# A hybrid decoder layer on one core: the base-rotor table stored with its 16 positions innermost, a left sum of the first feed-forward moved to VectorE, and side work every 2.75 matmul triples

## The chip, the core and the metric

The kernel runs on one core of a Trainium2 chip. The core has five engines with queues of their own: TensorE (PE in the profile; its weight loads are PEld), VectorE (DVE), ScalarE (ACT), GpSimd (POOL) and SyncE (SP), which here issues the DMAs. Each engine executes its instructions strictly in the order in which the program issues them and waits on semaphores for the others. The metric is the device time of one execution in microseconds, as a median over runs; lower is better.

## The reference, cut to what matters

One layer with 1024 tokens and width 1024: a feed-forward half-step, a mixer (short convolution and a diagonal state-space model side by side), a second feed-forward half-step, a final norm.

```python
h = modulate(rms_norm(x, ffn1_norm[l]), sh1, sc1)
x = x + 0.5 * g1[:, None, :] * swiglu(h, ffn1_w_gate[l], ffn1_w_up[l], ffn1_w_down[l])

h = modulate(rms_norm(x, mix_norm[l]), sh2, sc2)
proj = h @ w_in[l]
...
y_ssm = s5_mixer(u, lambda_re[l], lambda_im[l], log_dt[l], ssm_b_re[l], ssm_b_im[l],
                 ssm_c_re[l], ssm_c_im[l], ssm_d[l], glu_w[l], glu_b[l])
...
x = x + g2[:, None, :] * (y_mix @ w_out[l])

h = modulate(rms_norm(x, ffn2_norm[l]), sh3, sc3)
x = x + 0.5 * g3[:, None, :] * swiglu(h, ffn2_w_gate[l], ffn2_w_up[l], ffn2_w_down[l])
return rms_norm(x, final_norm)
```

Two things that depend on no activation are needed later: the modulation vectors, `silu(cond) @ w_mod + b_mod`, and the tables of the state-space model, among them the rotors, powers of `exp(i * lambda_im * dt)` for each of 32 groups of channels, with 64 states.

## The kernel before

**Arithmetic.** Every matmul of two matrices is done as three in reduced format: each operand is split into a high part and a low part, and `mm3` (line 306) issues high times high, high times low, low times high. Such a triple is the unit of the kernel's own clock. The activation's split is a cast on ScalarE and a subtraction on VectorE (`split_act`); a weight's split (tile `w`, from the loaded tile `raw`) is the same pair over 1024 columns.

**The first feed-forward.** The 2816 hidden columns are handled in 11 groups of 256 (names `fa0` to `fa10`), the 1024 tokens in two halves of 512. Groups 0 to 5 are direct: `gate_up` (line 1015) computes for each of two tiles the gate product (`fa2g`, ...) and the up product (`fa2u`, ...) for both halves, 64 triples in all; `gu_evac` takes them out of PSUM (Silu on ScalarE into `sg`, the product `af` on VectorE, then the split `a`). `down_both` (line 1027) multiplies by the down weights, 32 triples (`fa2d`, ...): 16 output tiles of six matmuls each, each taken out by one VectorE instruction that adds it to the residual `x`. All these products share six PSUM banks (`mm_ps`, line 229), so a new tile waits until an older one has been taken out. Groups 6 to 10 use a scheme with seven block products in place of eight (`seven`). It needs sums of activation blocks, made by `combos` (line 483): S1, S2 and S3 with VectorE additions during group 5, then, once group 5's projections are issued, the fourth left sum S4 = A12 − S2. In the code before, the three additions of S4 for each of four tiles (two recombinations of a split pair, `f12` and `s2`, and their difference) run on GpSimd, and the split into the tile `h1S` is done by ScalarE and VectorE as elsewhere. On GpSimd also run the sums of weight blocks (tile `sums`, lines 158 to 160).

**Side work.** While groups 0 to 4 run, a generator `side1` (line 997) is stepped by the clock: `Clock.tick` (line 67) is called at each triple and takes one step of the generator every `period` triples. The period is 4 at first, 3 during `gate_up` of groups 1 to 4 and 8 during their `down_both`. The generator first runs `ssm_base` (line 772): small VectorE instructions that make `lam`, `pw`, `tab` and two rotor tables, `base` (tile `rb`, 16 positions by 32 groups) and `step` (tile `rs`, 8 positions by 32 groups), by repeated doubling. Then come eight batches of `ssm_batch` (line 916), four channel groups each: products `bb`, `cl`, `bl` on VectorE, two groups of small matmuls on TensorE (`kp` and `tp`, which read `cl` and `bl`), copies to DRAM, three `mod_block`s (two reductions of a loaded 1024-wide tile `wm` each, on VectorE), and four products of `step` with `base` (`rot` and `rott`) with a sum for each pair. Each step ends at a `yield`.

**Order.** The program is written in this order, but a scheduler in the framework decides where each instruction stands in its engine's queue; after that the order is fixed. So the clock's steps decide roughly, and the scheduler exactly, what stands ahead of an eviction on VectorE or of a matmul on TensorE.

**Pools.** `sb` lives through the side work, `sb1` only through `ssm_base`; the pool `bp` of the batches takes the room of `sb1` afterwards.

Of the kernel before, what the change touches and what calls it, by code (L numbers as in the profile page):

```python
# [13 lines left out]
F32 = mybir.dt.float32  # L14
# [40 lines left out]
class Clock:  # L55
# [1 line left out]


    def __init__(self, period):
        self.now, self.period, self.n = 0, period, 0  # L60
        self.due, self.side = [], deque()

    def after(self, ticks, fn):
# [3 lines left out]
    def tick(self):  # L67
        self.now += 1
        while self.due and self.due[0][0] <= self.now:
            self.due.pop(0)[2]()  # L70
        if self.now % self.period == 0:
            self.step()

    def step(self):
# [142 lines left out]
def hymba_layer(ctx: ExitStack, tc, x_d, wm1_d, wmod_d, gu1_d, gs1_d, wd1_d, win_d, wout_d, glu_d, gu2_d, gs2_d, wd2_d, cols_d, cond_d, lam_d, bc_d, out_d):  # L217
# [265 lines left out]
    def combos(act, name, homes, engine=None):  # L483

        blocks.clear()
        while act[1] is None or len(act[1]) < KT:
            yield
        (a11, a12), (a21, a22) = [(act[h][:4], act[h][4:]) for h in range(2)]
        blocks.update(A11=a11, A12=a12, A22=a22, S1=[], S2=[], S3=[], S4=[])
        G_ = engine or V  # L490
        for k in range(4):
            f22, f21, f11 = whole(a22[k], f"f22_{k}", V), whole(a21[k], f"f21_{k}", V), whole(a11[k], f"f11_{k}", V)
            V.tensor_tensor(out=f22[:], in0=f21[:], in1=f22[:], op=ALU.add)
            blocks["S1"].append(split_act(f22[:], f"{name}S1_{k}", homes[0]))
            yield
            V.tensor_tensor(out=f21[:], in0=f11[:], in1=f21[:], op=ALU.subtract)
            V.tensor_tensor(out=f11[:], in0=f22[:], in1=f11[:], op=ALU.subtract)
            blocks["S2"].append(split_act(f11[:], f"{name}S2_{k}", homes[1]))
            yield
            blocks["S3"].append(split_act(f21[:], f"{name}S3_{k}", homes[2]))  # L500
            yield
        while "free" not in blocks:
            yield
        for k in range(4):
            f12, s2 = whole(a12[k], f"f12_{k}", G_), whole(blocks["S2"][k], f"s2_{k}", G_)
            yield
            G_.tensor_tensor(out=f12[:], in0=f12[:], in1=s2[:], op=ALU.subtract)
            blocks["S4"].append(split_act(f12[:], f"{name}S4_{k}", homes[3]))
            yield
# [262 lines left out]
    def ssm_base(sb1):  # L772
# [100 lines left out]
        V.tensor_tensor(out=r8[:], in0=w[0], in1=w[0], op=ALU.mult)  # L873
        V.tensor_scalar(out=ro[1][hi], in0=ro[1][hi], scalar1=-1.0, scalar2=None, op0=ALU.mult)
        cur = (ro[0], ro[1])
        base = [sb.tile([P, 16, G], F32, tag=f"rb{i}", name=f"rb{i}") for i in range(2)]
        step = [sb.tile([P, 8, G], F32, tag=f"rs{i}", name=f"rs{i}") for i in range(2)]

        def doubled(nm):
# [12 lines left out]
        for tab, cnt in ((base, 16), (step, 8)):  # L892
            V.memset(tab[0][:, 0, :], 1.0)
            V.memset(tab[1][:, 0, :], 0.0)
            n = 1
            while n < cnt:
                by = tuple(a.unsqueeze(1).to_broadcast([P, n, G]) for a in cur)
                cmul(sb1, 
                    tuple(t[:, n : 2 * n, :] for t in tab), tuple(t[:, 0:n, :] for t in tab), by, [P, n, G], f"t{cnt}_{n}"
                )  # L900
                doubled(f"c{cnt}_{n}")
                yield
                n *= 2
        yield
        zero = sb1.tile([CH, 112], F32, name="zero")
        V.memset(zero[:], 0.0)
        mk4 = mk_d[:].rearrange("b p (g c) -> p b g c", g=GB)
        for t in range(1, TAU):
            for b in range(NB):
# [1 line left out]
                    mk4[t * CH : (t + 1) * CH, b, :, 0 : t * CH],  # L911
                    zero[:, 0 : t * CH].unsqueeze(1).to_broadcast([CH, GB, t * CH]),
                )
        ssm.update(q=(qr, qi), tabs=tabs, base=base, step=step, lam=lam)

    def ssm_batch(b):
        bp = bps[0]
        gs = slice(b * GB, (b + 1) * GB)
        prm = bp.tile([P, 4, GB, CH], F32, tag="prm", name=f"prm{b}")
        SP.dma_start(prm[:], bc_d[b])  # L920
        bb = bp.tile([P, 2, GB, CH], F32, tag="bb", name=f"bb{b}")
        q = tuple(a[:, gs].unsqueeze(2).to_broadcast([P, GB, CH]) for a in ssm["q"])
        cmul(bp, (bb[:, 0], bb[:, 1]), (prm[:, 0], prm[:, 1]), q, [P, GB, CH], f"bb{b}")
        p1, p2, e1, e2 = ssm["tabs"]

        def bt(name):
            return bp.tile([P, 576], F32, tag="bt", name=name, bufs=4)

        def comb(dst, n, lam, src, op, nm):

            t = bt(nm)[:, : GB * n * CH].rearrange("p (g n c) -> p g n c", g=GB, n=n)
            la = [a[:, 0:n, gs].rearrange("p n g -> p g n").unsqueeze(3).to_broadcast([P, GB, n, CH]) for a in lam]
            sc = [a.unsqueeze(2).to_broadcast([P, GB, n, CH]) for a in src]
            V.tensor_tensor(out=dst, in0=la[0], in1=sc[0], op=ALU.mult)
            V.tensor_tensor(out=t, in0=la[1], in1=sc[1], op=ALU.mult)
            yield
            V.tensor_tensor(out=dst, in0=dst, in1=t, op=op)

        cl = bt(f"cl{b}")
        cl4 = cl[:].rearrange("p (g n c) -> p g n c", g=GB, n=9)  # L940
        yield from comb(cl4, 9, (p1, p2), (prm[:, 2], prm[:, 3]), ALU.add, f"clt{b}")
        SP.dma_start(mo_d[b].rearrange("p (g m) -> p g m", g=GB), cl4[:, :, 1:9, :].rearrange("p g n c -> p g (n c)"))
        bl = bt(f"bl{b}")
        bl4 = bl[:, :512].rearrange("p (g n c) -> p g n c", g=GB, n=8)
        yield from comb(bl4, 8, (e1, e2), (bb[:, 0], bb[:, 1]), ALU.add, f"blt{b}")
        yield from mod_block()

        kp = sm([CH, 512], f"kp{b}")
        for g in range(GB):
            T.matmul(  # L950
                kp[:, g * P : (g + 1) * P], lhsT=bl4[:, g, 7, :], rhs=cl4[:, g, 0:8, :].rearrange("p n c -> p (n c)"), start=True, stop=True
            )
        tp = sm([P, 512], f"tp{b}")
        for g in range(GB):
            T.transpose(tp[:, g * P : (g + 1) * P], bl[:, g * P : (g + 1) * P], ident[:])
        yield from mod_block()
        kc = bt(f"kc{b}")
        kc3 = kc[:CH, :512].rearrange("p (g m) -> p g m", g=GB)
        A.copy(kc[:CH, :512], kp[:])
        dg = bt(f"dg{b}")  # L960
        dg3 = dg[:CH, : GB * CH].rearrange("p (g m) -> p g m", g=GB)
        V.tensor_tensor(
            out=dg3,
            in0=ident[:CH, :CH].unsqueeze(1).to_broadcast([CH, GB, CH]),
            in1=ssm["lam"][:CH, 3, gs].unsqueeze(2).to_broadcast([CH, GB, CH]),
            op=ALU.mult,
        )
        V.tensor_tensor(out=kc3[:, :, 0:CH], in0=kc3[:, :, 0:CH], in1=dg3, op=ALU.add)
        yield
        mk3 = mk_d[b].rearrange("p (g m) -> p g m", g=GB)  # L970
        for t in range(TAU):
            SP.dma_start(mk3[t * CH : (t + 1) * CH, :, t * CH :], kc3[:, :, : P - t * CH])
        mi = bt(f"mi{b}")
        A.copy(mi[:, :512], tp[:])
        SP.dma_start(mi_d[b], mi[:, :512])
        yield from mod_block()

        rot = [bt(f"rot{b}_{i}") for i in range(2)]
        t = [bt(f"rott{b}_{i}") for i in range(2)]

        def v3(a):
            return a[:, :512].rearrange("p (g m i) -> p g m i", g=GB, m=8)

        bs = [a[:, :, gs].rearrange("p i g -> p g i").unsqueeze(2).to_broadcast([P, GB, 8, 16]) for a in ssm["base"]]
        st = [a[:, :, gs].rearrange("p m g -> p g m").unsqueeze(3).to_broadcast([P, GB, 8, 16]) for a in ssm["step"]]
        for i, op in enumerate((ALU.subtract, ALU.add)):
            V.tensor_tensor(out=v3(rot[i]), in0=st[0], in1=bs[i], op=ALU.mult)
            V.tensor_tensor(out=v3(t[i]), in0=st[1], in1=bs[1 - i], op=ALU.mult)
            yield
            V.tensor_tensor(out=rot[i][:, :512], in0=rot[i][:, :512], in1=t[i][:, :512], op=op)  # L990
            SP.dma_start((co_d, si_d)[i][b], rot[i][:, :512])
# [43 lines left out]
    for g in range(1, first_seven):  # L1035
        a_tiles = {}
        if g == first_seven - 1:
            while clock.side:
                clock.step()
            clock.period = 4  # L1040
            es1.close()
            movs["B"] = es1.enter_context(tc.tile_pool(name="movB1", bufs=12))
            clock.side.append(combos(act1, "h1", "BBBA", nc.gpsimd))
            ws.retire(ring1)
        else:
            clock.period = 3
        gate_up(act1, f"fa{g}", a_tiles)
        if g < first_seven - 1:
            clock.period = 8
        else:  # L1050
            blocks["free"] = True
            ring1_open.close()
            sums_open = sums_opened()
        down_both(a_tiles, f"fa{g}")
# [399 lines left out]
```

## Time and profile before

| | us |
|---|---|
| time, median of 3 runs | 1777.08 (1774.29 to 1778.9) |
| time of the profiled execution | 1774.26 |
| its span, first to last instruction | 1772.5 |
| TensorE busy | 1720.6 (97%) |
| VectorE busy | 1210.2 (68%) |
| ScalarE busy | 490.9 (28%) |
| GpSimd busy | 222.8 (13%) |
| mean granted TensorE clock | 0.995 |

How to read the rows: a row of a timeline has the start (us from the span's start), the length, the engine, the line of the kernel, the operation, output tile `<-` input tiles, shapes and `xN` for N instructions merged; in brackets stands the idle time before it and what ended it. The recorded lengths of neighbours on one engine overlap a little, so the distance from one start to the next is what an instruction costs its queue. Rows of groups give the busy time, the mean length in ns and the idle time before. All work of this kernel goes through one recording helper, so nearly every row shows line 101; the tiles' names tell the rows apart. A share of TensorE of 97% doesn't mean that it runs at its peak: matmuls are pipelined.

### The profile page before, as it was taken

Reading aid. Unit: us, or ns where it says so; the run is one execution under the profiler, and the core shown is the slowest. Engines: PE = TensorE matmul, PEld = TensorE weight load, DVE = VectorE, ACT = ScalarE, POOL = GpSimd, SP = SyncE. Lnnn points to the kernel's source line nnn. Section 1 sums busy time; section 2 is a strip of 40 time slices with the busy share of each in tenths; the row PEclk is TensorE's granted clock in tenths of the full one; section 3 lists DMA queues with packets and bytes.
Section 4 is the critical chain, followed back from the end, with each engine's and each line's share of the span. In section 5 each row is a group of like instructions: output and inputs, shape, how many; then the busy total and the mean of one; then the engine's idle time right before and its main releaser. Section 6 shows DMA issues by size and latency. Waiting matters only on the chain.

```text
span 1772.5 us, 20086 instructions
## 1 busy us (share of the span) xinstructions
PE 1720.6 (97%) x7772; PEld 1417.9 (80%) x7772; DVE 1210.2 (68%) x2182; ACT 490.9 (28%) x750; POOL 222.8 (13%) x143
## 2 busy tenths in 40 slices
PE   4999999999999999999999999999999999999997
PEld 3787888888888888878787888788888888888886
DVE  7999999987566556563566738975665565556646
ACT  4311212122222323331213424332223223222331
POOL 0000000005212121210000022022112111212211
PEclk9999999999999999999999999999999999999998
DMA  7624666520111211215663010111111111111102
GB/s 308 233 71 158 205 210 216 193 73 24 48 48 48 72 48 62 99 40 162 193 194 107 25 48 25 48 67 52 49 48 51 50 64 52 48 48 51 69 24 95
DMA packets 58737, 165.02 MB, mean 93 GB/s; under 512 B 14353, under 2 KB 29969, under 8 KB 43922
## 3 DMA queue, kind: packets, MB, share of 16 engines
q1 hardware_dynamic: 58642, 163.74, 27.1%
q8 instruction: 61, 1.00, 0.2%
q14 instruction: 34, 0.28, 0.0%
HBM read 140.64 MB, written 18.87 MB: 90 GB/s over the span
## 4 chain that ended last, share of the span: by engine, by line
PE 78%; DVE 14%; DMA 3%; issue 1%; ACT 1%; POOL 1%; SPq 1%; DVEq 0%; ACTq 0%; POOLq 0%
PE wo L101 5%; DVE w L101 2%; PE u L101 2%; PE b L101 2%; PE fb10d L101 2%; DVE x L101 2%; PE fa10d L101 2%; PE v L101 1%; PE fb0u L101 1%; PE c L101 1%; PE fa4u L101 1%; PE fa5u L101 1%; PE fb0g L101 1%; PE fb8d L101 1%; PE fb7d L101 1%; PE fb6d L101 1%
## 5 line engine op out<-in xcount | busy, mean ns | idle before, releaser
L101 ACT CAST w<-raw 128x1024 fp32r<-128x1024 f32 (+1 forms) x203 | 171.6, 860 | 505.4 <-POOL raw L159 58.1
L101 DVE TENSOR_TENSOR w<-raw,w 128x1024 fp32r<-128x1024 f32 (+1 forms) x203 | 208.5, 1040 | 57.6 <-ACT w L101 55.1
L158 POOL TENSOR_TENSOR sums<-raw 128x1024 f32<-128x1024 f32 x30 | 77.5, 2582 | 1092.7 <-DVE w L101 668.7
L101 DVE TENSOR_TENSOR w<-sums,w 128x512 fp32r<-128x512 f32 x90 | 59.7, 688 | 47.3 <-ACT w L101 47.0
L101 ACT CAST w<-sums 128x512 fp32r<-128x512 f32 x90 | 52.8, 619 | 133.8 <-PE fa6d L101 9.7
L101 DVE CUSTOM_DVE_ANT_0 wm<-wm,cact 128x1024 f32<-128x1024 f32 x48 | 58.0, 1212 | 0.8 <-DMA wm<-in_wmod 0.8
L101 PE MATMUL v<-h,w 128*128 128x512 f32 x192 | 46.9, 395 | 0.0
L101 PE MATMUL c<-h,w 128*128 128x512 f32 x192 | 46.6, 394 | 0.0
L101 PE MATMUL wo<-oa,w 128*128 128x512 f32 x192 | 45.4, 391 | 0.6 <-DVE w L101 0.6
L101 PE MATMUL u<-h,w 128*128 128x512 f32 x192 | 44.9, 392 | 0.8 <-DVE w L101 0.8
L101 PE MATMUL b<-h,w 128*128 128x512 f32 x192 | 45.6, 393 | 0.0
L101 PE MATMUL wo<-ob,w 128*128 128x512 f32 x192 | 45.2, 391 | 0.0
L101 PEld LDWEIGHTS u<-h,w 128*128 128x128 f32 x192 | 35.6, 188 | 9.1 <-DVE w L101 1.2
L101 PEld LDWEIGHTS wo<-oa,w 128*128 128x128 f32 x192 | 35.8, 188 | 8.7 <-DVE w L101 1.1
L101 PEld LDWEIGHTS wo<-ob,w 128*128 128x128 f32 x192 | 35.8, 188 | 7.4
L101 PE MATMUL p<-h,w 128*128 128x512 f32 x144 | 37.2, 418 | 4.3 <-DVE h L101 2.2
L101 PEld LDWEIGHTS b<-h,w 128*128 128x128 f32 x192 | 35.5, 188 | 7.2
L101 PEld LDWEIGHTS c<-h,w 128*128 128x128 f32 x192 | 35.4, 188 | 7.0
L101 PEld LDWEIGHTS v<-h,w 128*128 128x128 f32 x192 | 35.3, 188 | 7.0
L159 POOL TENSOR_TENSOR raw<-sums,raw 128x512 f32<-128x512 f32 x30 | 40.3, 1343 | 2.4
L339 POOL TENSOR_TENSOR n3aq<-n3aq,n3aq 128x512 f32<-128x512 f32 x5 | 6.5, 1292 | 271.3 <-ACT n3aq L101 271.2
L160 POOL TENSOR_TENSOR sums<-raw 128x512 f32<-128x512 f32 x30 | 40.2, 1340 | 2.4
(1095 smaller groups left out, 4015.0 us busy)
## 6 DMA issues: line engine op xcount, KB each, us to landing
raw<-in_gs SPq DMA_DIRECT2D x30, 1024.0 KB, 4.8
wm<-in_wmod SPq DMA_DIRECT2D x24, 1024.0 KB, 5.0
raw<-in_wd SPq DMA_DIRECT2D x22, 1024.0 KB, 4.8
raw<-in_gu SPq DMA_DIRECT2D x14, 1024.0 KB, 5.0
mw<-in_wm SPq DMA_DIRECT2D x8, 1024.0 KB, 8.7
raw<-in_win SPq DMA_DIRECT2D x8, 1024.0 KB, 5.9
x<-in_x SPq DMA_DIRECT2D x8, 512.0 KB, 6.7
mw<-in_wmod SPq DMA_DIRECT2D x4, 1024.0 KB, 4.9
```

Source lines behind the costliest of these rows:

```text
L101: r = getattr(self.engine, name)(*args, **kw)
L158: self.G.tensor_tensor(out=f[:, :1024], in0=r[:, 512:1536], in1=r[:, :1024], op=ALU.subtract)
L159: self.G.tensor_tensor(out=r[:, 512:1024], in0=f[:, 512:1024], in1=r[:, :512], op=ALU.add)
L160: self.G.tensor_tensor(out=f[:, 1024:], in0=r[:, 1536:], in1=r[:, 512:1024], op=ALU.subtract)
L339: nc.gpsimd.tensor_tensor(out=a, in0=a, in1=sq[:, :n], op=ALU.add)
```

## The change

Three edits, and one that the third needs.

- The base rotors are still built as 16 positions by 32 groups, now in the pool `sb1`. When they and the step table are complete, two ScalarE copies write them into a second table `baset` (tile `rt`), 32 groups by 16 positions, which takes their place in `sb`. The four products of a batch read it so that the innermost 16 elements lie next to each other; before, they lay 32 elements apart.
- `combos` of the first feed-forward is called without an engine, so that the twelve additions for S4 are VectorE's. The second feed-forward's call was so already.
- The period during `gate_up` of groups 1 to 4 is 2.75 in place of 3.
- For that the clock counts the triples since the last step, and carries a remainder of up to one triple over, where before it tested the count for divisibility. With whole periods it steps as before, apart from the phase at a change of period.

```diff
     def __init__(self, period):
-        self.now, self.period, self.n = 0, period, 0
+        self.now, self.period, self.n, self.since = 0, period, 0, 0
         self.due, self.side = [], deque()
...
-        if self.now % self.period == 0:
+        self.since += 1
+        if self.since >= self.period:
+            self.since = max(0, min(self.since - self.period, 1))
             self.step()
...
         cur = (ro[0], ro[1])
-        base = [sb.tile([P, 16, G], F32, tag=f"rb{i}", name=f"rb{i}") for i in range(2)]
+        base = [sb1.tile([P, 16, G], F32, tag=f"rb{i}", name=f"rb{i}") for i in range(2)]
+        baset = [sb.tile([P, G, 16], F32, tag=f"rt{i}", name=f"rt{i}") for i in range(2)]
...
                 n *= 2
+        for i in range(2):
+            A.copy(baset[i][:], base[i][:].rearrange("p i g -> p g i"))
         yield
...
-        ssm.update(q=(qr, qi), tabs=tabs, base=base, step=step, lam=lam)
+        ssm.update(q=(qr, qi), tabs=tabs, base=baset, step=step, lam=lam)
...
-        bs = [a[:, :, gs].rearrange("p i g -> p g i").unsqueeze(2).to_broadcast([P, GB, 8, 16]) for a in ssm["base"]]
+        bs = [a[:, gs, :].unsqueeze(2).to_broadcast([P, GB, 8, 16]) for a in ssm["base"]]
...
-            clock.side.append(combos(act1, "h1", "BBBA", nc.gpsimd))
+            clock.side.append(combos(act1, "h1", "BBBA"))
             ws.retire(ring1)
         else:
-            clock.period = 3
+            clock.period = 2.75
```

## The prediction

> **What bounds the kernel now.** I began with the page's busy shares and slices, then asked what TensorE waited for between 100 and 460 us, the only part the change reaches; behind it the issue order on every engine is unchanged.
>
> ```profile
> span 1772.5 us, 20086 instructions
> ...
> PE 1720.6 (97%) x7772; PEld 1417.9 (80%) x7772; DVE 1210.2 (68%) x2182; ACT 490.9 (28%) x750; POOL 222.8 (13%) x143
> ...
> DVE  7999999987566556563566738975665565556646
> ```
> ```profile
> PE fa1d L101 <- DVE x L101: 3.2, 3, 2.5
> PE fa5d L101 <- DVE x L101: 1.5, 2, 1.0
> PE kp L101 <- DVE bl L101: 1.0, 2, 0.6
> PE fa2d L101 <- DVE x L101: 0.2, 1, 0.2
> ```
>
> The reader should see two things. TensorE sets the end, so only its gaps can be won. And its gaps here add up to 5.9 us, all of them waits for VectorE, which the slices show full from slice 2 to 8: VectorE is the only engine through which the change can act. How late it is at the first of those gaps (fa1d, the down projection of group 1) shows in the two engines' timelines side by side:
>
> ```profile
> 150.05 6.96 PE L101 MATMUL fa1d<-fa_0a,w 128*128 128x512 f32 x30
> 159.53 4.37 PE L101 MATMUL fa1d<-fa_0a,w 128*128 128x512 f32 x12 [2.52 <-DVE x L101]
> ...
> 165.18 1.05 PE L101 MATMUL kp<-cl,bl 128*16 128x128 f32 x8
> ...
> 166.57 0.95 PE L101 MATMUL fa1d<-fa_0a,w 128*128 128x512 f32 x3
> ...
> 174.44 5.07 PE L101 MATMUL fa1d<-fa_1a,w 128*128 128x512 f32 x21 [0.30 <-DVE x L101]
> 179.35 5.83 PE L101 MATMUL fa2g<-h,w 128*128 128x512 f32 x25
> ...
> 191.83 11.04 PE L101 MATMUL fa2u<-h,w 128*128 128x512 f32 x48
> 202.71 10.59 PE L101 MATMUL fa2g<-h,w 128*128 128x512 f32 x46
> ```
> ```profile
> 156.91 1.22 DVE L101 CUSTOM_DVE_ANT_0 wm<-wm,cact 128x1024 f32<-128x1024 f32 x1
> ...
> 158.06 0.68 DVE L101 TENSOR_TENSOR fa_1a<-fa_1af,fa_1a 128x512 fp32r<-128x512 f32 x1
> ...
> 158.73 0.74 DVE L101 SCALAR_TENSOR_TENSOR x<-fa1d,gate,x 128x512 f32<-128x512 f32 x1
> 159.39 0.21 DVE L101 TENSOR_TENSOR bb<-prm,qr 128x64 f32<-128x64 f32 x1
> ...
> 163.41 0.15 DVE L101 SCALAR_TENSOR_TENSOR scl<-scl,cols 128x2 f32<-128x2 f32 x1
> 163.48 0.74 DVE L101 SCALAR_TENSOR_TENSOR x<-fa1d,gate,x 128x512 f32<-128x512 f32 x1
> ```
>
> 48 matmuls take 202.71 − 191.83 = 10.88 us, 0.2267 us each; the group kp and tp takes 166.57 − 165.18 = 1.39. The 96 matmuls of fa1d with one such group need 23.2 us, and had 179.35 − 150.05 = 29.3: 6.1 lost. VectorE goes on from row to row without a gap, an eviction (x) each 0.66 us, a product wm each 1.15.
>
> **The table.** Sixteen-wide runs of the base table are now read one element after the other.
>
> ```profile
> L101 DVE CUSTOM_DVE_ANT_0 wm<-wm,cact 128x1024 f32<-128x1024 f32 x44 | 53.2, 1214 | 0.8 <-DMA wm<-in_wmod 0.8
> ...
> L101 DVE TENSOR_TENSOR rot<-rs,rb 128x512 f32<-128x512 f32 x16 | 17.9, 1119 | 1.3 <-PE tp L101 1.3
> L101 DVE TENSOR_TENSOR rott<-rs,rb 128x512 f32<-128x512 f32 x16 | 17.9, 1118 | 2.0 <-DMA mk_d<-kc 1.9
> ...
> L101 DVE TENSOR_TENSOR bl<-tab,bb 128x512 f32<-128x512 f32 x8 | 5.5, 682 | 0.0
> ```
>
> The bl products have just the pattern that the rot products get: one source repeated sixteen times, the other in runs of sixteen. So 32 x (1.119 − 0.682) = 14.0 us of VectorE go; at worst none. The price is two copies on ScalarE with one strided side, between 0.6 us (its plain 128x512 copies) and 1.1 (VectorE's strided product); I take 0.6, since ScalarE's own row is the nearer, and nothing hangs on it: the table is complete at 142.5, and ScalarE is free for 8.7 us there. One instruction queues behind them, the activation fa_1sg, which slips from 140.4 to 143.7; its reader on VectorE runs at 153.8.
>
> ```profile
> 141.76 0.75 DVE L101 TENSOR_TENSOR rb<-t,t 128x256 f32<-128x256 f32 x2
> ...
> 153.83 0.68 DVE L101 TENSOR_TENSOR fa_1af<-fa_1sg,fa1u 128x512 f32<-128x512 f32 x1
> ```
> ```profile
> 140.37 0.59 ACT L101 ACTIVATE fa_1sg<-fa1g 128x512 f32<-128x512 f32 x1
> 149.64 0.62 ACT L101 CAST fa_0a<-fa_0af 128x512 fp32r<-128x512 f32 x1 [8.68 <-DVE fa_0af L101]
> ```
>
> **Side work every 2.75.** A projection stage of 64 triples hands out 23.3 steps instead of 21.3, and the down stage keeps its 4: 8% more side work for each group. A batch cost VectorE about 19 us (all its rows in the view of the wm, rot and bl rows come to some 150 us for eight batches, wm, rot and rott alone to 89) and now 1.75 less, 9%. So from group 2 to group 4 VectorE is as full as before, and the 14 us become an earlier end of the side work (its last step falls on triple 432, was 472), where TensorE waited for nothing. That is where the large saving goes.
>
> At fa1d it isn't neutral: the rot products come too late to help, and more side work has been handed out. In the changed order the first eviction of fa1d has ahead of it one more wm and the whole run from bb to scl: 158.73 + 1.15 + (163.48 − 159.39) = 163.97, and its bank is free at 164.7. TensorE has six banks, fills them with 36 matmuls (two groups of three are drawn forward), and stands from 150.05 + 36 x 0.2267 = 158.2 to 164.7: 6.5 us where it was 2.5. Some of this comes back, for the evictions behind follow more closely; what decides is the eleventh eviction, whose bank the first tile of fa2g needs. Between the first and it stand ten evictions (6.6), rot products and sums (3.6), two wm (2.3), cl, bl and small ones (5.0): 17.5 us, so it starts at 181.5 and ends at 182.2. TensorE's own 60 remaining matmuls and kp from 164.7 take 15.0, or 16.7 with half a clock for a while (below): 181.4, just inside. fa2g starts near 182.5, not 179.35: **+3.2 us**.
>
> The clock after the stall, by stretches (length, busy TensorE, weight load, VectorE, ScalarE, POOL, then granted clock, DMA share, GB/s):
>
> ```profile
> 159.00:161.00 2.00, 1.47 (x6) 1.25 (x7) 2.00 (x9) 0.00 (x0) 0.00 (x0) 0.97 0.98 406
> 161.00:164.00 3.00, 2.90 (x7) 1.71 (x6) 3.00 (x6) 0.00 (x0) 0.00 (x0) 0.50 0.49 208
> 164.00:167.00 3.00, 2.72 (x17) 1.98 (x18) 3.00 (x7) 0.73 (x2) 0.00 (x0) 0.95 0.49 131
> ```
>
> After 2.5 us of waiting the clock was halved for some 3.4 us, which cost 1.7; I charge the same once for the longer stall. [...]
>
> **What comes back in groups 2 to 4.** From 179.35 to the start of fa5d at 431.62 lie 1056 matmuls and seven kp groups: 239.4 + 9.7 = 249.1 of 252.3 us, 3.2 lost, of which the table of waits names 1.2. In the changed order each kp stands earlier in TensorE's queue, but bl earlier on VectorE too; by adding up VectorE's rows bl is ready 0 to 10 us ahead of kp in each case. I take **−1.8**; the bounds are 0 and −3.2.
>
> **The fourth left sum on VectorE.** Twelve POOL instructions go, and with them VectorE's slowing at fa5d:
>
> ```profile
> 431.62 6.96 PE L101 MATMUL fa5d<-fa_0a,w 128*128 128x512 f32 x30
> ...
> 445.80 9.87 PE L101 MATMUL fa5d<-fa_1a,w 128*128 128x512 f32 x42 [1.00 <-DVE x L101]
> 455.50 2.88 PE L101 MATMUL fa6gA<-h,w 128*128 128x512 f32 x12
> ```
> ```profile
> 431.82 0.69 DVE L101 TENSOR_TENSOR fa_1af<-fa_1sg,fa5u 128x512 f32<-128x512 f32 x1 [2.83 <-PE fa5u L101]
> ...
> 436.58 1.78 DVE L101 TENSOR_TENSOR h1S<-f,h1S 128x512 fp32r<-128x512 f32 x1
> 438.28 2.71 DVE L101 SCALAR_TENSOR_TENSOR x<-fa5d,gate,x 128x512 f32<-128x512 f32 x4
> 440.92 4.17 DVE L101 TENSOR_TENSOR h1S<-f,h1S 128x512 fp32r<-128x512 f32 x3
> 445.00 2.72 DVE L101 SCALAR_TENSOR_TENSOR x<-fa5d,gate,x 128x512 f32<-128x512 f32 x4
> ```
>
> The four h1S sums took 1.78 and 4.17 for three here, 1.5 us each on the mean, against the 0.69 of fa_1af. VectorE gets twelve instructions of 0.60 (7.2 us), spread among the evictions. In the changed order the first eviction has fa_1af, f, w, fa_1a and s ahead of it: 431.82 + 4 x 0.60 + 1.15 = 435.4, was 438.3; the fifth begins at 440.4, was 445.0, and TensorE wants its bank by 431.62 + 10 x 1.36 = 445.2 (six matmuls for each tile). All sixteen keep over 1 us in hand. S4 itself is first read six products of 12 x 0.2267 us after 455.5, at 471.8. fa5d took 455.50 − 431.62 = 23.9 us for 21.8 of matmuls: **−2.1**, bounds 0 and −2.1.
>
> **Sum.** 3.2 − 1.8 − 2.1 = −0.7 us on the profiled execution's own time of 1774.26 (span 1772.5 and 1.8 around it): 1773.6. That execution lies at the lower edge of the three timed runs, 2.8 below their median of 1777.08; on the median the forecast is 1776.4: no change that can be told. A measurement here tells a change from none at about 0.3%, 5.3 us.
>
> **Rivals.**
> 1. Slower: kp becomes the wait. TensorE runs in order, and kp now stands after 39, 99, 216, 312, 439, 531, 666 and 770 matmuls of the stretch, where it was 45, 121, 238, 348, 465, 565, 726 and 825. At the fifth and sixth my margin is 0.6 and 1.2 us; from a VectorE later than that by 2 us on, say through a product waiting for its transfer, six kp groups stand for about 1.5 each: +3.2 + 9 − 2.1 = +10, 1787. For it: waits for bl exist already (1.0). Against: VectorE saves 1.75 a batch before each of them.
> 2. Faster: the stall at fa1d doesn't grow, because the evictions behind close up as fast as the longer wait opens, and the rest is recovered in full: −3.2 − 2.1 = −5.3, 1771.8. Against it: the eleventh eviction.
> [...]
> 4. The table doesn't do what it says: rot stays at 1.12 because the repeated source costs it. Then 8% more side work meets a full VectorE, up to 14 us too much of it, and with half of that on TensorE it is +3.2 + 7 − 2.1 = +8: 1785. The bl row speaks against.
>
> **How the numbers follow.** Forecast 0.55; rival 1 0.15, rival 2 0.17, rival 3 0.09, rival 4 0.04. Rival 2 lies at the bound, and most of it counts as faster with the scatter of the runs, as does a little of the forecast: faster 0.17. Rivals 1 and 4 are slower, with an edge of the forecast's own upper bound (3.2 + 1.7 = +4.9): 0.22. Same 0.61. The forecast's own range is 1771.8 to 1782; with the scatter and part of the rivals 1769.5 to 1783.5.
>
> **What would show it.** rot and rott near 0.68 us; TensorE's wait at fa1d near 6.5 us in one piece, then a clock of 0.5; fa2g starting 3 us later; no fa5d wait for x; no POOL rows named f or s there; the last rot near 345 us, with nothing gained from it. The prediction falls if the first eviction of fa1d comes before 162, or if kp waits add up to more than 3 us.

## The result, and the profile after

The changed kernel takes 1779.05 us (median of 20 runs, 1776.85 to 1783.05); the kernel before, run beside it, 1777.15 us (20 runs, 1774.29 to 1779.71). The medians lie 1.9 us apart; the ratio, estimated from all the runs, is 1.0014, 95% interval 1.0007 to 1.002: 2.5 us slower, between 1.2 and 3.6. That lies within 0.3% of no change and inside the range of the prediction, but on the other side of zero: the forecast was 0.7 us faster.

The page of the changed kernel: the span, the busy shares of TensorE (PE) and VectorE (DVE), and VectorE's slices.

```profile
span 1778.7 us, 20093 instructions
...
PE 1719.8 (97%) x7772; PEld 1417.9 (80%) x7772; DVE 1196.6 (67%) x2194; ACT 493.2 (28%) x752; POOL 204.8 (12%) x131
...
DVE  6999999976666556563566737975655565556546
```

VectorE has 13.6 us less to do (1210.2 before), GpSimd 18.0 less. TensorE's busy time is the same, and the time is longer: the saving on VectorE was real and stood beside the path. What TensorE waited for between 100 and 475 us (in all, times, longest):

```profile
PE fa1d L103 <- DVE x L103: 6.6, 2, 6.4
PE fa2g L103 <- DVE x L103: 1.6, 1, 1.6
PE kp L103 <- DVE bl L103: 0.8, 1, 0.8
PE kp L103 <- DVE mods L103: 0.2, 1, 0.2
```

The waits for fa5d are gone; fa1d waits twice as long as before (3.2), and a wait at fa2g is new. TensorE's and VectorE's timelines around fa1d:

```profile
150.76 8.32 PE L103 MATMUL fa1d<-fa_0a,w 128*128 128x512 f32 x36
165.53 1.65 PE L103 MATMUL fa1d<-fa_0a,w 128*128 128x512 f32 x3 [6.45 <-DVE x L103]
167.10 1.89 PE L103 MATMUL kp<-cl,bl 128*16 128x128 f32 x8
168.92 1.09 PE L103 MATMUL tp<-ident,bl 128*128 128x128 f32 x4
169.69 2.41 PE L103 MATMUL fa1d<-fa_0a,w 128*128 128x512 f32 x9
171.94 2.89 PE L103 MATMUL fa1d<-fa_1a,w 128*128 128x512 f32 x12
175.02 8.46 PE L103 MATMUL fa1d<-fa_1a,w 128*128 128x512 f32 x36 [0.19 <-DVE x L103]
185.03 0.96 PE L103 MATMUL fa2g<-h,w 128*128 128x512 f32 x3 [1.56 <-DVE x L103]
```
```profile
159.49 1.22 DVE L103 CUSTOM_DVE_ANT_0 wm<-wm,cact 128x1024 f32<-128x1024 f32 x1
...
164.73 0.74 DVE L103 SCALAR_TENSOR_TENSOR x<-fa1d,gate,x 128x512 f32<-128x512 f32 x1
...
169.68 0.21 DVE L103 TENSOR_TENSOR kc<-kc,dg 16x64 f32<-16x64 f32 x1 [1.51 <-ACT kc L103]
170.05 0.69 DVE L103 TENSOR_TENSOR rot<-rs,rt 128x512 f32<-128x512 f32 x1 [0.16 <-PE tp L103]
...
184.23 0.75 DVE L103 SCALAR_TENSOR_TENSOR x<-fa1d,gate,x 128x512 f32<-128x512 f32 x1
```

One wm more and a whole run of small products now stand ahead of the first eviction at 164.73, and TensorE stands for 6.45 us with its six banks full. The row to notice is kc: VectorE, the engine that is late, itself stands idle for 1.51 us. It waits for ScalarE's copy of kp, and kp is queued on TensorE behind the three matmuls that had waited. The eviction at 184.23 is the eleventh; fa2g starts when it is done, at 185.03.

The view of stretches (length, busy PE, weight load, DVE, ACT, POOL, then granted clock, DMA share, GB/s) shows the clock behind the wait, and behind the second one:

```profile
162.00:165.00 3.00, 0.00 (x0) 0.00 (x0) 3.00 (x7) 0.00 (x0) 0.00 (x0) 0.67 0.43 178
165.00:168.00 3.00, 2.47 (x8) 1.48 (x9) 3.00 (x6) 0.00 (x0) 0.00 (x0) 0.50 0.48 131
168.00:171.00 3.00, 3.00 (x14) 2.26 (x13) 1.33 (x4) 1.17 (x2) 0.00 (x0) 0.69 0.00 0
171.00:174.00 3.00, 3.00 (x15) 2.46 (x14) 3.00 (x6) 0.00 (x0) 0.00 (x0) 1.00 0.36 116
...
186.00:189.00 3.00, 3.00 (x19) 2.44 (x20) 3.00 (x6) 0.57 (x1) 0.00 (x0) 1.00 0.21 25
```

The twelve matmuls and one kp group from 165.53 to 171.94 took 6.4 us, where 12 x 0.2267 + 1.39 = 4.1: half the clock cost 2.3 us. The first three stretches, 0.67, 0.50 and 0.69, come from some 6.8 us at half clock (3 x (0.33 + 0.50 + 0.31) / 0.5), twice the 3.4 of the kernel before; it began while TensorE still waited. Behind the 1.56 us at fa2g the clock stayed at 1.00.

The rot groups and the stage fa5d, where things went as said:

```profile
L103 DVE TENSOR_TENSOR rot<-rs,rt 128x512 f32<-128x512 f32 x16 | 10.9, 681 | 0.2 <-PE tp L103 0.2
L103 DVE TENSOR_TENSOR rott<-rs,rt 128x512 f32<-128x512 f32 x16 | 10.9, 681 | 0.0
```
```profile
437.56 11.04 PE L103 MATMUL fa5d<-fa_0a,w 128*128 128x512 f32 x48
448.44 11.04 PE L103 MATMUL fa5d<-fa_1a,w 128*128 128x512 f32 x48
459.31 1.07 PE L103 MATMUL fa6gA<-h,w 128*128 128x512 f32 x4
```

From the starts of these rows, and the same rows of every other kernel, come the stage times below, in us: fa1d from its first matmul to the first of fa2g, groups 2 to 4 (with the projections of group 5) from there to the first of fa5d, fa5d from there to the first of fa6gA.

| kernel | period in group 1 / 2 to 4 | time, median | ratio to before, 95% | fa1d | groups 2 to 4 | fa5d | the three |
|---|---|---|---|---|---|---|---|
| before | 3 / 3 | 1777.15 | | 29.30 | 252.27 | 23.88 | 305.45 |
| changed | 2.75 / 2.75 | 1779.05 | 1.0014 (1.0007 to 1.002) | 34.27 | 252.53 | 21.75 | 308.55 |
| table_sum_p3 | 3 / 3 | 1773.09 | 0.997 (0.9958 to 0.9981) | 28.22 | 250.98 | 21.76 | 300.96 |
| period_only | 2.75 / 2.75 | 1786.16 | 1.004 (1.0028 to 1.0053) | 35.60 | 255.09 | 23.88 | 314.57 |
| sum_only | 3 / 3 | 1776.88 | 0.9992 (0.9983 to 1.0001) | 29.29 | 253.11 | 21.76 | 304.16 |
| table_only | 3 / 3 | 1776.23 | 0.9992 (0.9983 to 1.0) | 28.33 | 250.98 | 23.84 | 303.15 |
| g1_p3 | 3 / 2.75 | 1775.14 | 0.9987 (0.9977 to 0.9998) | 28.23 | 253.41 | 21.76 | 303.40 |
| g1_275_p3 | 2.75 / 3 | 1780.89 | 1.0015 (1.0006 to 1.0024) | 34.70 | 252.67 | 21.76 | 309.13 |
| g1_p4 | 4 / 2.75 | 1769.83 | 0.9955 (0.994 to 0.997) | 26.36 | 250.68 | 21.76 | 298.80 |
| g1_p4_p3 | 4 / 3 | 1769.96 | 0.9954 (0.9942 to 0.9967) | 26.41 | 250.98 | 21.76 | 299.15 |
| before_g1_p4 | 4 / 3 | 1774.98 | 0.9983 (0.9974 to 0.9992) | 26.42 | 253.45 | 23.89 | 303.76 |
| kc_later | 2.75 / 2.75 | 1779.23 | 1.0012 (1.0002 to 1.0022) | 34.02 | 251.99 | 21.76 | 307.77 |
| kc_pool | 2.75 / 2.75 | 1779.87 | 1.0018 (1.0007 to 1.0028) | 31.54 | 255.55 | 21.76 | 308.85 |

What lies behind fa6gA took 1316.9 to 1320.7 us in these single executions, without a pattern by kernel, so the stage times say more than the spans. Each ratio is to runs of the kernel before in the same session. The stage times are single executions too: from fa1d to fa5d, sum_only issues the same instructions in the same order as the kernel before on TensorE, VectorE and ScalarE, and yet its groups 2 to 4 took 0.8 us longer, with one kp waiting for 0.9. A difference below 1 us in that column is not certain. Changed against before they add up to +5.0 + 0.3 − 2.1 = +3.1 us, which agrees with the 2.5 measured. The 14 us of shorter rot products are found in no stage of the changed kernel.

### The profile page after: what moved, and what is told of

It is laid out like the page before. It is cut to its first block, busy times and chain, and to the rows that moved or that the text cites. A ratio compares the mean times of both kernels' runs of the same rounds, so it can differ in the third digit from the quotient of the medians.

```text
span 1778.7 us, 20093 instructions
## 1 busy us (share of the span) xinstructions
PE 1719.8 (97%) x7772; PEld 1417.9 (80%) x7772; DVE 1196.6 (67%) x2194; ACT 493.2 (28%) x752; POOL 204.8 (12%) x131
## 4 chain that ended last, share of the span: by engine, by line
PE 81%; DVE 14%; DMA 3%; ACT 1%; issue 1%; SPq 0%; POOL 0%; DVEq 0%; ACTq 0%; POOLq 0%
PE wo L103 5%; DVE w L103 2%; PE u L103 2%; PE b L103 2%; PE fb10d L103 2%; DVE x L103 2%; PE fa10d L103 2%; PE c L103 1%; PE fa2g L103 1%; PE fb0u L103 1%; PE fa3d L103 1%; PE fa4g L103 1%; PE fb8d L103 1%; PE fb7d L103 1%; PE fb6d L103 1%; PE fb5d L103 1%
## 5 line engine op out<-in xcount | busy, mean ns | idle before, releaser
L103 PEld LDWEIGHTS p<-h,w 128*128 128x128 f32 x144 | 27.8, 196 | 13.6 <-DVE h L103 4.9
```

Of the source, the lines that this page charges most:

```text
L103: r = getattr(self.engine, name)(*args, **kw)
```

## The experiments

### The three edits apart

**table_sum_p3**: the changed kernel with the old period.

```diff
-            clock.period = 2.75
+            clock.period = 3
```

> The changed kernel with the period back at 3: table and sum alone. Theory (the period alone moves the evictions of fa1d back): VectorE's queue has the first eviction of fa1d where it was, so TensorE waits there about 2.9 us in pieces as before, not 6.5 in one; no fa5d wait; 2 us faster than the kernel before (-1.5 to -3). Rival (the table's ScalarE copies or its new place cost something at fa1d): the long wait at fa1d stays, and it is as slow as the changed kernel, +2.5 us.

Measured: 1773.09 us (1771.5 to 1774.52), ratio 0.997. No kp wait is left, fa1d takes 28.2 us and groups 2 to 4 take 1.3 less than before. The long wait at fa1d is gone as the theory says, but the gain is more than its 1.5 to 3 us. So the table and the sum together are worth 5 us, and the period turns that into a loss.

**period_only**: the kernel before with the changed clock and period 2.75, the old table, S4 on GpSimd.

```diff
-        if self.now % self.period == 0:
-            self.step()
+        self.since += 1
+        if self.since >= self.period:
+            self.since = max(0, min(self.since - self.period, 1))
+            self.step()
...
-            clock.period = 3
+            clock.period = 2.75
```

> The kernel before with the period of 2.75 and its counter alone. Theory: the same first eviction as in the changed kernel and rot products of 1.12 us behind it, so fa2g starts about 1.7 us later still (fa1d stage +6.5 against before), the fa5d wait stays, and with 8% more side work on a VectorE that was full, waits for bl or x in groups 2 to 4 come on top: +6 to +12 us. Rival (the period is harmless, the loss is elsewhere): within 1 us of before.

Measured: 1786.16 us, ratio 1.004. fa1d takes 6.3 us more than before, and in groups 2 to 4 the waits of kp add up to 3.4 us. The price of the period is +9.1 us by the stage times on the old table and 308.55 − 300.96 = +7.6 on the new one: a cheaper rot takes off little of it.

**sum_only**: the kernel before with one word out.

```diff
-            clock.side.append(combos(act1, "h1", "BBBA", nc.gpsimd))
+            clock.side.append(combos(act1, "h1", "BBBA"))
```

> The kernel before with the fourth left sum on VectorE alone. Theory: all else as before, fa5d in 21.8 us in place of 23.9: -2.1 us. Rival (the fa5d wait is a wait for something else and stays, or moves into fa6): no change.

Measured: 1776.88 us, ratio 0.9992 (to 1.0001). fa5d falls by 2.1 us to 21.76, with no other edit in the kernel; in the whole time this can't quite be told from nothing.

**table_only**: the changed kernel with period 3 and S4 back on GpSimd.

```diff
-            clock.side.append(combos(act1, "h1", "BBBA"))
+            clock.side.append(combos(act1, "h1", "BBBA", nc.gpsimd))
...
-            clock.period = 2.75
+            clock.period = 3
```

> The kernel before with the transposed table alone, period 3, sums on GpSimd. Theory: rot and rott at 0.68 us, 14 us of VectorE less, and nearly nothing of it on the end: the evictions 5 to 11 of fa1d come up to 1.8 us earlier, worth 0 to 1 us, and the first wait at fa1d stays at 2.5: 0 to -1 us. Rival (VectorE's load is what TensorE waits for in groups 1 to 4): the 3.2 us lost in groups 2 to 4 come back too, -3 to -5 us.

Measured: 1776.23 us, ratio 0.9992. The 14 us that VectorE saves give 1.0 us at fa1d and 1.3 in groups 2 to 4, where kp waits no longer: more than the theory's 0 to 1, less than the rival's 3 to 5. This run and table_sum_p3 keep the new counter, and in both the last two kp groups stand 9 matmuls earlier than before; what that is worth was not measured.

### The period, by groups

**g1_p3**: the changed kernel, with 3 in group 1.

```diff
-            clock.period = 2.75
+            clock.period = 3 if g == 1 else 2.75
```

> The changed kernel with period 3 in group 1 and 2.75 in groups 2 to 4. Theory (the whole price of 2.75 is paid at fa1d, where VectorE is already late): the stretch from the start of fa1d to the start of fa2g falls from 34.3 to 28.2 us as in the run with period 3 everywhere, groups 2 to 4 stay at 252.5 us: 1779.05 - 6.0 = 1773.0 us. Rival (2.75 costs wherever kp stands in front of a full VectorE): groups 2 to 4 grow by 2 us or more, with kp waits above 2 us in sum: 1775 us or more.

Measured: 1775.14 us, 2 us above the theory. fa1d fell to 28.23 as it said; groups 2 to 4 did not stay at 252.5. TensorE's waits there:

```profile
PE fa1d L103 <- DVE x L103: 2.6, 1, 2.6
PE fa2d L103 <- DVE x L103: 1.6, 1, 1.6
PE kp L103 <- DVE bl L103: 0.8, 3, 0.5
```

An eviction of fa2d and three kp waited, 2.4 us, just the difference to table_sum_p3's 250.98. The rival's sizes, 2 us of growth over 252.5 and kp waits above 2 us, weren't reached either (0.9 and 0.8). So here 2.75 has a second, smaller price behind group 1.

**g1_275_p3**: the counterpart, 2.75 in group 1 and 3 behind it.

```diff
-            clock.period = 2.75
+            clock.period = 2.75 if g == 1 else 3
```

> The changed kernel with period 2.75 in group 1 and 3 in groups 2 to 4, the counterpart of the run with 3 in group 1 and 2.75 behind it (1775.1 us, 28.2 us from fa1d to fa2g, 253.4 us in groups 2 to 4). Theory (two separate prices: about 5 us at fa1d from group 1, about 2 us in groups 2 to 4 from the kp that stand earlier in TensorE's queue): 34.3 us from fa1d to fa2g, about 251 us in groups 2 to 4: 1777.4 us. Rival (the time in groups 2 to 4 is the aftermath of group 1's stall): groups 2 to 4 at 253 us, 1779 us.

Measured: 1780.89 us, as bad as the changed kernel, so group 1 carries nearly all of the loss. Groups 2 to 4 took 252.67, 1.7 above table_sum_p3, as the rival said, and the rows say why. TensorE's timeline, then its stretch, right behind the wait at fa2g:

```profile
185.03 0.96 PE L103 MATMUL fa2g<-h,w 128*128 128x512 f32 x3 [2.12 <-DVE x L103]
185.92 1.68 PE L103 MATMUL kp<-cl,bl 128*16 128x128 f32 x8
```
```profile
186.00:189.00 3.00, 3.00 (x14) 2.21 (x15) 3.00 (x6) 0.57 (x1) 0.00 (x0) 0.53 0.20 27
```

Here the second wait (2.12 us) did halve the clock again, which the 1.56 of the changed kernel did not; kp took 1.68 where it takes 1.05. It is the aftermath of group 1, in the form of a second slow stretch.

**g1_p4**: fewer steps in group 1.

```diff
-            clock.period = 2.75
+            clock.period = 4 if g == 1 else 2.75
```

> The changed kernel with period 4 in group 1 and 2.75 in groups 2 to 4. Theory (VectorE's work ahead of the evictions of fa1d sets the stall): the first eviction has 6.8 us of rows ahead of it in place of 13.2, the eleventh 19.4 in place of 30.8, so the wait at fa1d falls from 6.4 to about 1 us and the stretch from fa1d to fa2g to 25 to 26.5 us (23.2 is TensorE's own); the five steps not handed out in group 1 are run later, where nothing waits for them: about 1771 us. Rival A (a short wait halves the clock as a long one does): 1.7 us more, 1772.7 us. Rival B (the deferred side work meets a full VectorE in groups 2 to 4 and makes kp wait): groups 2 to 4 above 255 us, 1775 us or more.

Measured: 1769.83 us (1768.94 to 1771.61), ratio 0.9955: faster than both kernels. fa1d's rows, and the stretches behind them:

```profile
158.61 4.41 PE L103 MATMUL fa1d<-fa_0a,w 128*128 128x512 f32 x18 [1.32 <-DVE x L103]
...
164.61 0.50 PE L103 MATMUL fa1d<-fa_1a,w 128*128 128x512 f32 x1 [0.91 <-DVE x L103]
...
176.68 8.55 PE L103 MATMUL fa2g<-h,w 128*128 128x512 f32 x37
```
```profile
159.00:162.00 3.00, 3.00 (x15) 2.40 (x14) 3.00 (x11) 0.00 (x0) 0.00 (x0) 1.00 0.41 175
162.00:165.00 3.00, 2.09 (x9) 1.27 (x7) 3.00 (x6) 0.00 (x0) 0.00 (x0) 1.00 0.28 87
```

The wait came in two pieces of 1.32 and 0.91 and the clock never left 1.00, so rival A fell. In groups 2 to 4, still at 2.75, nothing waits: rival B fell too, and with it any fixed price of 2.75 there. A reading that fits, and that no run tests by itself, is that a kp waits according to how much side work group 1 left to VectorE and to where the kp lands.

**g1_p4_p3**: 4 in group 1, 3 behind it.

```diff
-            clock.period = 2.75
+            clock.period = 4 if g == 1 else 3
```

> The changed kernel with period 4 in group 1 and 3 in groups 2 to 4. Up to fa2g its order is that of the run with 4 and 2.75 (26.4 us from fa1d to fa2g); the side work ends later, still inside group 4. Theory (with 2.75 after a relieved group 1 no kp waited, so there is nothing more to win): groups 2 to 4 at 250.5 us, 1769.8 us. Rival (2.75 costs about 2 us there whatever came before): 248.5 us, 1768 us.

Measured: 1769.96 us (1768.65 to 1770.21), groups 2 to 4 at 250.98, with one kp wait of 0.4: the theory holds, there is next to nothing more to win there.

**before_g1_p4**: the kernel before, with period 4 in group 1 alone.

```diff
-            clock.period = 3
+            clock.period = 4 if g == 1 else 3
```

> The kernel before with period 4 in group 1 and nothing else changed: the base table as it was, the fourth sum on GpSimd. Rows ahead of the first and the eleventh eviction of fa1d are 6.8 and 19.4 us, as in the changed kernel with period 4. Theory (the gain of period 4 is made at fa1d alone and needs no shorter rot): 26.4 us from fa1d to fa2g, where before had 29.3, groups 2 to 4 at 252.3: 1777.15 - 2.9 = 1774.2 us. Rival (with rot at 1.12 us the deferred side work makes kp wait): groups 2 to 4 at 255 us or more, 1777 us.

Measured: 1774.98 us, ratio 0.9983. fa1d gains 2.9 us as with the new table, but in groups 2 to 4 some goes back, to the waits of kp, the first line here. The fa1d waits are in g1_p4_p3 too (2.3 in all), and those of fa5d belong to S4 on GpSimd:

```profile
PE kp L101 <- DVE bl L101: 2.8, 2, 1.5
PE fa1d L101 <- DVE x L101: 2.3, 2, 1.4
PE fa5d L101 <- DVE x L101: 1.5, 2, 1.0
```

Theory and rival are each half right. Here the table earns its keep: with rot at 0.68, g1_p4_p3 needs 2.5 us less in groups 2 to 4 for the deferred steps.

### VectorE waiting for TensorE

**kc_later**: the copy of tp, its transfer and two wm products ahead of the sum kc, which came behind them.

```diff
         A.copy(kc[:CH, :512], kp[:])
+        mi = bt(f"mi{b}")
+        A.copy(mi[:, :512], tp[:])
+        SP.dma_start(mi_d[b], mi[:, :512])
+        yield
+        yield from mod_block()
         dg = bt(f"dg{b}")
...
         V.tensor_tensor(out=kc3[:, :, 0:CH], in0=kc3[:, :, 0:CH], in1=dg3, op=ALU.add)
-        yield
...
-        mi = bt(f"mi{b}")
-        A.copy(mi[:, :512], tp[:])
-        SP.dma_start(mi_d[b], mi[:, :512])
-        yield from mod_block()
```

> The changed kernel with the sum kc (VectorE, reads ScalarE's copy of kp) issued behind the next products of wm instead of ahead of them; the work ahead of the first and of the eleventh eviction of fa1d is the same. Theory (VectorE waits for kp, which runs at half clock behind the stall, and the eleventh eviction pays it): the wait of kc falls from 1.5 us to about 0.4, the wait at fa2g from 1.6 to 0.3 us, the stretch from fa1d to fa2g from 34.3 to about 33.0 us: 1777.8 us. Rival (the eleventh eviction is late through the sheer number of rows ahead of it): no change of that stretch, 1779 us; if the sums rot then wait for the transfers of kc instead, 1780 us.

Measured: 1779.23 us, fa1d 34.02: a miss. The number is the rival's, but the run decides nothing: the wait didn't shrink, it changed its name. VectorE's rows:

```profile
168.63 0.21 DVE L103 TENSOR_TENSOR dg<-ident,lam 16x64 f32<-16x64 f32 x1 [1.04 <-issue]
169.39 0.69 DVE L103 TENSOR_TENSOR rot<-rs,rt 128x512 f32<-128x512 f32 x1 [0.55 <-PE tp L103]
```

1.04 + 0.55 = 1.59 us of idle time, as the 1.51 + 0.16 of the changed kernel. For the 1.04 at dg the view names no cause, but kp's rows end at 168.54, just ahead of it. The tiles of a batch take turns in four buffers; rot doesn't read tp, so it presumably waits for a buffer that tp reads, and does so whether or not kc stands ahead of it. The run took no wait away and so tells nothing of its price.

**kc_pool**: the sum kc on GpSimd.

```diff
-        V.tensor_tensor(out=kc3[:, :, 0:CH], in0=kc3[:, :, 0:CH], in1=dg3, op=ALU.add)
+        nc.gpsimd.tensor_tensor(out=kc3[:, :, 0:CH], in0=kc3[:, :, 0:CH], in1=dg3, op=ALU.add)
```

> The changed kernel with the sum kc on GpSimd, so that VectorE waits for no copy of kp at all. In its order the eleventh eviction of fa1d also has 2.7 us less work ahead of it (28.1 in place of 30.8), the first the same. Theory: the wait at the first bank of fa1d stays at 6.4 us, the wait at fa2g goes and the stretch from fa1d to fa2g is TensorE's own behind the stall: 34.3 - 1.6 = 32.7 us, 1777.4 us. Rival (the waits of kc on VectorE are idle time that nobody pays): 34.3 us, 1779 us.

Measured: 1779.87 us. At fa1d more than the theory had: 31.54 us, with no wait at fa2g. But VectorE still stood for tp, 1.38 us ahead of rot, so it was the 2.7 us of work fewer ahead of the eleventh eviction that took the wait at fa2g away. Some 0.5 us more is the clock: the same twelve matmuls and kp group took 170.82 − 164.91 = 5.9 us here, not 6.4. The gain was given back in group 2. TensorE's row there, and the stretch behind it:

```profile
238.73 1.03 PE L103 MATMUL kp<-cl,bl 128*16 128x128 f32 x8 [1.93 <-DVE bl L103]
```
```profile
240.00:243.00 3.00, 3.00 (x10) 2.32 (x9) 3.00 (x5) 1.00 (x2) 0.31 (x1) 0.50 0.69 274
```

TensorE waited 1.93 us for bl, and the clock halved behind it. Groups 2 to 4 took 3.0 us more. That VectorE's own wait of 1.67 us prolonged fa1d is thus worked out from rows; no run removed it.

## Why the prediction was wrong, step by step

**The first bank: right.** One wm and the run from bb to scl came ahead of the first eviction as added up: it began 13.97 us after the stage, 13.92 was said; the wait was 6.45 us in one piece where 6.5 stood, and the clock was 0.50 behind it, though for twice as long as charged.

**The eleventh eviction: the step that failed.** The prediction had it start at 181.5, "just inside" TensorE's own 181.4, and took +3.2 us from that. It began at 184.23. Of the 2.7 us, 0.7 is the later start of the stage (150.76), 1.51 + 0.16 is VectorE waiting for kp and tp, and 0.3 is spread over other rows. The list of rows ahead of an eviction held only VectorE's durations, with the sentence that VectorE goes from row to row without a gap. That held in the kernel before by a hair. Its rows of ScalarE and of VectorE:

```profile
166.26 0.58 ACT L101 COPY kc<-kp 16x512 f32<-16x512 f32 x1 [11.10 <-DVE dg L101]
```
```profile
166.87 0.21 DVE L101 TENSOR_TENSOR kc<-kc,dg 16x64 f32<-16x64 f32 x1
```

The copy ended at 166.84 and the sum began at 166.87: no idle time, and no margin either. Behind the longer wait kp and tp ran wholly at half clock and took 169.69 − 167.10 = 2.59 us where before they took 1.39: what VectorE had caused came back to VectorE. TensorE's own side was short too: half the clock cost 2.3 us, not the 1.7 taken over from before. The prediction charged one slow stretch of some 3.4 us for the long stall; the clock stood at half for some 6.8 us, of which TensorE worked through 4.3. The stage took +5.0.

**Groups 2 to 4: the other half of the miss.** −1.8 was taken from "3.2 lost"; the result is +0.3. All the runs with a new table and next to nothing late (250.7 to 251.0) show that only 1.3 of the 3.2 could be had, what the table of waits named (1.2); the other 1.9 is in every kernel, so it was an error in my price for a matmul or a kp group, not a loss. Most of it can be found: in table_sum_p3 the matmul ahead of a kp group and the one behind it mostly take 0.32 us from start to start in place of 0.2267, some 1.3 us for seven groups. And 2.75 took back 252.53 − 250.98 = 1.5, 1.0 of it in waits of kp, the largest through the mishap that the first rival named, a product waiting for a transfer. VectorE's row, then TensorE's, in the changed kernel:

```profile
266.70 0.69 DVE L103 TENSOR_TENSOR blt<-tab,bb 128x512 f32<-128x512 f32 x1 [1.26 <-DMA si_d<-rot]
```
```profile
269.36 1.03 PE L103 MATMUL kp<-cl,bl 128*16 128x128 f32 x8 [0.82 <-DVE bl L103]
```

**fa5d: right.** −2.13 us for −2.1, in the changed kernel and in sum_only alone; 96 matmuls run without a wait, and the h1S products there take 0.68 us with GpSimd's rows gone, where they took 1.5 on the mean in the kernel before.

**The table: right in itself.** 0.681 us for both products, and the first evictions of fa1d have none of them ahead. Its copies on ScalarE took 1.06 us each, not 0.6, and fa_1sg slipped to 145.1, which nobody waited for. But what the prediction made of the saving didn't come: the last sum of rot ran at 364.5 us (363.5 before), not near 345. Nor was VectorE as full as before: from fa2g to that sum it stood idle for 18.5 us, where it was 6.3: most of the 14 us became idle time of VectorE.

**The rivals.** The first (kp waits, 1787) had its mechanism and not its size: 1.0 us of kp waits in place of 9; without the table it comes out at once, 3.4 us in period_only. The second (no longer wait at fa1d) fell. The third stood for a second slow stretch behind the eleventh eviction, whose 1.7 us are also in the forecast's own upper bound of +4.9 and which no row of the kernel before shows; it didn't occur in the changed kernel (1.00 behind 1.56 us) and did in g1_275_p3 (0.53 behind 2.12). In the changed kernel the second 3.4 us at half clock followed directly on the first. The fourth fell by the rot rows.

So the mechanism was right in the main (the period pays at fa1d, fa5d gains, the table saves mostly beside the path), and two terms were wrong: +3.2 measured +5.0, and −1.8 measured +0.3, the other sign. And the edit that was called neutral outside fa1d is the one that costs: the period loses 7.6 us of which the other two edits win 4.5 back.

## What to carry to other kernels

Background work that is metered into a saturated engine must be metered by what the critical engine next needs from it: here fewer steps before the first late eviction (4 in place of 2.75) brought nearly 10 us by the stage times (308.55 − 298.80), though more room had been made on VectorE for more steps. When you add up the rows ahead of a due instruction, look in that list for rows that wait for the engine you are delaying: behind a stall they don't cost their duration alone. And a "loss" that is a span less a price per instruction is only as good as the price; take as recoverable what the view of waits names.

## What the runs showed of the hardware that was not expected

What the granted clock did behind a wait of TensorE can't be read off the one case in the kernel before (2.52 us of waiting, then 0.50 for some 3.4 us). Behind single waits of 0.91 and 1.32 (g1_p4), 1.56 (the changed kernel), 1.63 (g1_p3 at fa2d) and 1.79 us (period_only at fa1d) it stayed at 1.00; behind 1.93 (kc_pool) and 2.12 us (g1_275_p3) it was 0.50 for some 3.4 us, and around the 6.45 of the changed kernel for some 6.8. But the length of the wait alone doesn't decide it, as TensorE's row at fa2g in kc_later and the stretches there show (columns as above):

```profile
184.34 0.96 PE L103 MATMUL fa2g<-h,w 128*128 128x512 f32 x3 [2.01 <-DVE x L103]
```
```profile
183.00:186.00 3.00, 1.66 (x10) 1.18 (x11) 3.00 (x6) 0.41 (x1) 0.00 (x0) 1.00 0.38 116
186.00:189.00 3.00, 3.00 (x17) 2.38 (x15) 3.00 (x6) 1.16 (x2) 0.00 (x0) 1.00 0.48 68
```

Here the clock stayed at 1.00 behind 2.01 us, where it was 0.50 behind the 1.93 of kc_pool. No run was made to tell the two apart, so what else enters was not shown. For a wait of some 2 us both outcomes were measured, with and without the slow stretch, which cost 1.7 us in the kernel before.
